# A two-layer decoder trunk in float32: four gated products of the feed-forwards, on GpSimd instead of VectorE

## The chip, the core and the metric

One core of one Trainium2 chip runs the whole program. The metric is the device time of one execution in microseconds (us), the median of several runs of the same program. The engines run side by side, each through its own queue in order, and wait for each other by semaphores: TensorE (PE, matrix products), VectorE (DVE), ScalarE (ACT), GpSimd (POOL) and SyncE (SP), which issues most of the transfers between HBM and the on-chip memory (SBUF). PE writes its results to PSUM.

## The reference

A sequence of 1024 tokens of width 1024 goes through two layers. Each has a token mixer (a gated linear recurrence in the first, sliding-window attention in the second) and then a gated feed-forward with a causal depthwise convolution of width 3. The change lies in the feed-forward alone:

```python
FFN_DIM = 2816
def conv_ffn(h, w_in, conv_w, conv_b, w_out):
    u = h @ w_in                                   # (S, 2 * FFN_DIM)
    u = causal_depthwise_conv(u, conv_w) + conv_b  # each column by itself, over 3 tokens
    a, b = jnp.split(u, 2, axis=-1)
    return (jax.nn.silu(a) * b) @ w_out
...
h = layer_norm(ALPHA * h + mix, ln_mix_g[layer], ln_mix_b[layer])
ff = conv_ffn(h, ffn_w_in[layer], ffn_conv_w[layer], ffn_conv_b[layer], ffn_w_out[layer])
h = layer_norm(ALPHA * h + ff, ln_ffn_g[layer], ln_ffn_b[layer])
```

The gated product is `silu(a) * b`.

## The kernel before

**The up-projection** (class `Up`, once per layer). The 5632 columns of `u` are made in 22 *chunk pairs* `fc`: 128 columns of `a` and the 128 columns of `b` that belong to them, for all 1024 tokens, with the columns on the partitions. A pair is a 2 x 2 block product made with seven block products (Strassen's scheme in Winograd's form) instead of eight. They are numbered, and run in the order 1, 2, 6, 7, 4, 5, 3; for pairs 0 and 1 they are interleaved and the products 4 and 5 come first, while layer norms of the last tokens are still under way. Each block product is 12 matmuls of 512 columns: four slices of the contraction, each in three passes (lines 194 to 196), since operands are split into a high part, which ACT makes by a cast (line 221), and a low part, the rest, which DVE subtracts (line 169). The third pass (L196) is the one that reads the low part of the weights.

**The weights of a pair** are loaded by SP (L416) into two of four raw buffers (rx0, rx1, rx2 and the last block of Y), split as they are (`weight_load`), then DVE forms the sums that the scheme needs (`weight_sums`, L425 to L428) and these are split in turn. The results lie in HL and HT. Even pairs use rx0 and rx1, odd pairs from 3 on rx2 and Y. So "L427 Y<-Y,rx2", "L428 rx2<-rx2,Y" and "L169 HL<-Y" belong to pair 3; that last one is the low part which its product 6 reads.

**Collecting a pair** (`collect`). Each block product is added from its PSUM bank into a tile C of Y (L451, L452 by ACT; L454 to L465 by DVE). After product 4 the half `a` is complete, after product 3 the half `b`. A complete half goes through the convolution: ACT makes its first tap with bias (L471), DVE adds the other two (L473, twice), for `a` ACT then takes silu (L476), and for `b` DVE multiplies the two halves (L478) and SP stores the product to HBM (L479, tile gd), where the down-projection fetches it. The half `a` lives in block 4 or 5 of Y (even or odd pair) until its store is done, the half `b` of every pair in block 6. So ACT's L471 for the next pair's `b` may only start when L478 has read block 6.

**PSUM.** A psmm tile is one bank; a psax tile is two banks. From pair 2 on the products go round eight banks, two of them in each psax tile.

**What sets the order.** PE's order is the order of the code. In the feed-forwards the orders of DVE, ACT, POOL and SP are made by a scheduler when the program is built, which estimates how long each instruction takes and places it by that; a change of one instruction's engine can therefore move others.

**GpSimd** has one operation in the feed-forwards: the power in the layer norm (L243, 128x1). Elsewhere it adds the bias in the attention (L1372, 128x512) and does one low part near the start (L169, 128x1024).

Of the kernel before, what the change touches and what calls it, by code (L numbers as in the profile page):

```python
# [14 lines left out]
ALU = mybir.AluOpType  # L15
# [92 lines left out]
def trunk(ctx: ExitStack, tc: tile.TileContext, a: dict, out: bass.AP):  # L108
    nc = tc.nc
# [232 lines left out]
    tt = nc.vector.tensor_tensor  # L342
# [6 lines left out]
    class Up:  # L349
# [97 lines left out]
        def collect(self, p, fc, ps):  # L447
            l, C = self.l, Y[:, 2 * (fc % 2):2 * (fc % 2) + 2, :]
            C11, C21, C12, C22 = C[:, 0, :512], C[:, 0, 512:], C[:, 1, :512], C[:, 1, 512:]
            if p == 1:  # L450
                nc.scalar.copy(C11, ps)  # L451
                nc.scalar.copy(C12, ps)  # L452
            elif p == 2:
                tt(C11, C11, ps, op=add)  # L454
            elif p == 6:
                tt(C12, C12, ps, op=add)
            elif p == 7:
                tt(C22, C12, ps, op=add)
            elif p == 4:
                tt(C21, C22, ps, op=add)  # L460
            elif p == 5:
                both = C[:, 1, :].rearrange("p (h n) -> p h n", h=2)
                tt(both, both, ps.unsqueeze(1).to_broadcast([P, 2, 512]), op=add)
            elif p == 3:
                tt(C12, C12, ps, op=add)  # L465
            if p in (4, 3):
                part = 0 if p == 4 else 1
                ci = fc + part * NF
                u, ca = C[:, part, :], Y[:, 4 + fc % 2, :]
                c = Y[:, 6, :] if part else ca  # L470
                nc.scalar.activation(c, u, AF.Identity, bias=cwt[:, l, 3, ci:ci + 1], scale=cwt[:, l, 2, ci:ci + 1])  # L471
                for sh in (1, 2):
                    nc.vector.scalar_tensor_tensor(c[:, sh:], u[:, :S - sh], cwt[:, l, 2 - sh, ci:ci + 1],  # L473
                                                   c[:, sh:], op0=ALU.mult, op1=ALU.add)
                if part == 0:
                    nc.scalar.activation(c, c, AF.Silu)  # L476
                else:
                    tt(ca, ca, c, op=ALU.mult)  # L478
                    nc.sync.dma_start(gd[:, fc, :], ca)  # L479

        def run(self, ready, down):
# [1080 lines left out]
```

## Time and profile before

| | |
|---|---|
| median of 3 runs | 2152.23 us (2151.32 to 2153.89) |
| the profiled execution | 2151.58 us |
| its span, first to last instruction | 2149.8 us |
| granted TensorE clock, mean | 0.999 |
| DVE, ACT, POOL: instructions | 2318, 1472, 143 |
| gated products (L478) on DVE | 44, 53.8 us in all, 1223 ns each |
| up-projection of layer 0, layer 1 | about 570 to 980 us, about 1520 to 1930 us |

How to read the rows below. The page gives each engine's busy time, and the span in 40 equal slices with the busy share of an engine in tenths. A row of who waits for whom has the engine and line that waited, the engine and line that ended the wait, the total, how many times, and the longest, in us. A row of the timeline has the start in us from the span's start, the duration in us, the engine, the line, the operation, what it writes and reads, the shape and the count; in brackets the idle time of that engine just before it and what ended it. PEld is PE's weight load, SPq a transfer's issue on SP. Matmuls overlap, so their start times tell more than their durations. A row of the chain of waits has the start, the time that this step has in the chain, and the instruction.

### The profile page before, as it was taken

To read this page: it belongs to the slowest core of one execution; us is meant where nothing else is said; L and a number is where in the kernel's file an instruction comes from. 1 tells how busy PE (TensorE), PEld (TensorE's weight loads), DVE (VectorE), ACT (ScalarE), POOL (GpSimd) and SP (SyncE) were. 2 spreads that over 40 slices of the span, in tenths; PEclk is the share of its full clock that TensorE was granted. 3 is DMA by queue.
4 is the path that set the end of the run, shared out by engine and by line. 5 is a ranking of instruction groups with operands and counts; after the bars stand their busy time and mean duration, and the time that the engine had idled before them with its cause. 6 is when DMAs were issued, how large, how long until landed. Compare 5 with 4: busy or idle time off the path is not lost.

```text
span 2149.8 us, 33060 instructions
## 1 busy us (share of the span) xinstructions
PE 2135.9 (99%) x13165; PEld 1809.0 (84%) x13165; DVE 1743.3 (81%) x2318; ACT 918.5 (43%) x1472; POOL 122.1 (6%) x143
## 2 busy tenths in 40 slices
PE   9999999999999999999999999999999999999998
PEld 9899999898888888888888888878888888888887
DVE  3877765577999999887978558969999899878986
ACT  3344434353444444434433256743544444444430
POOL 1000000001100000000001123311000000000002
PEclk9999999999999999999999999999999999999999
DMA  5755541123222222228854411133233222249662
GB/s 200 292 204 211 177 138 41 34 85 123 99 85 95 86 89 81 82 93 284 279 186 157 128 30 30 33 118 108 89 98 98 85 82 89 79 144 329 226 213 92
DMA packets 229842, 279.03 MB, mean 130 GB/s; under 512 B 29960, under 2 KB 158648, under 8 KB 226872
## 3 DMA queue, kind: packets, MB, share of 16 engines
q1 hardware_dynamic: 228736, 276.53, 38.5%
q8 instruction: 103, 1.69, 0.3%
q10 hardware_dynamic: 856, 0.37, 0.1%
q14 instruction: 51, 0.42, 0.1%
q0 software_dynamic: 96, 0.02, 0.0%
HBM read 213.94 MB, written 62.94 MB: 129 GB/s over the span
## 4 chain that ended last, share of the span: by engine, by line
PE 96%; DVE 2%; DMA 1%; issue 0%; ACT 0%; SPq 0%; DVEq 0%; ACTq 0%
PE psmm L194 20%; PE psmm L196 20%; PE psmm L195 20%; PE psax L194 9%; PE psax L196 9%; PE psax L195 9%; PE psax L200 3%; PE psmm L204 1%; PE psmm L200 1%; PE psax L204 1%; PE psax L1356 1%; DMA rx<-in_ffn_w_out_dram 1%; DVE T L169 0%; DVE Y L473 0%; PE psmm L688 0%
## 5 line engine op out<-in xcount | busy, mean ns | idle before, releaser
L194 PE MATMUL psmm<-T,HL 128*128 128x512 f32 x768 | 305.0, 397 | 0.0
L196 PE MATMUL psmm<-T,HL 128*128 128x512 f32 x768 | 299.4, 390 | 0.0
L195 PE MATMUL psmm<-T,HL 128*128 128x512 f32 x768 | 299.1, 389 | 0.0
L473 DVE SCALAR_TENSOR_TENSOR Y<-Y,cwt 128x1023 f32<-128x1023 f32 (+1 forms) x176 | 225.1, 1281 | 41.1 <-ACT Y L471 39.5
L221 ACT CAST HL<-rx 128x1024 fp32r<-128x1024 f32 (+1 forms) x151 | 152.0, 1009 | 200.8 <-PE psmm L195 46.9
L194 PE MATMUL psmm<-HL,T 128*128 128x256 f32 (+1 forms) x640 | 192.3, 300 | 0.9 <-issue 0.9
L196 PE MATMUL psmm<-HL,T 128*128 128x256 f32 (+1 forms) x640 | 189.8, 297 | 0.0
L195 PE MATMUL psmm<-HL,T 128*128 128x256 f32 (+1 forms) x640 | 189.6, 296 | 0.0
L169 DVE TENSOR_TENSOR HL<-rx,HL 128x1024 fp32r<-128x1024 f32 (+1 forms) x151 | 174.6, 1162 | 11.0 <-ACT HL L221 10.7
L196 PEld LDWEIGHTS psmm<-T,HL 128*128 128x128 f32 x768 | 144.1, 188 | 30.9
L194 PEld LDWEIGHTS psmm<-T,HL 128*128 128x128 f32 x768 | 144.3, 188 | 28.6
L195 PEld LDWEIGHTS psmm<-T,HL 128*128 128x128 f32 x768 | 144.4, 188 | 27.9
L471 ACT ACTIVATE Y<-Y,cwt 128x1024 f32<-128x1024 f32 x88 | 109.0, 1239 | 99.3 <-DVE Y L460 90.5
L194 PE MATMUL psax<-T,HL 128*128 128x512 f32 x352 | 137.3, 390 | 0.0
L196 PE MATMUL psax<-T,HL 128*128 128x512 f32 x352 | 137.0, 389 | 0.0
L195 PE MATMUL psax<-T,HL 128*128 128x512 f32 x352 | 137.0, 389 | 0.0
L195 PEld LDWEIGHTS psmm<-HL,T 128*128 128x128 f32 x640 | 122.3, 191 | 4.2 <-issue 1.0
L243 POOL TENSOR_TENSOR rs<-rs,nhalf 128x1 f32<-128x1 f32 x32 | 46.2, 1445 | 1398.7 <-DVE rs L242 1398.7
L194 PEld LDWEIGHTS psmm<-HL,T 128*128 128x128 f32 x640 | 122.3, 191 | 3.7 <-issue 0.4
L196 PEld LDWEIGHTS psmm<-HL,T 128*128 128x128 f32 x640 | 122.2, 191 | 3.5 <-DVE T L169 0.3
L169 DVE TENSOR_TENSOR HL<-raw,HL 128x1024 fp32r<-128x1024 f32 x51 | 62.2, 1222 | 71.9 <-ACT HL L176 71.8
L221 ACT CAST HT<-rx 128x1024 fp32r<-128x1024 f32 (+1 forms) x37 | 35.6, 962 | 113.9 <-DVE rx L427 74.3
(302 smaller groups left out, 5117.7 us busy)
## 6 DMA issues: line engine op xcount, KB each, us to landing
rx<-in_ffn_w_in_dram SPq DMA_DIRECT2D x136, 256.0 KB, 3.1
rx<-gd SPq DMA_DIRECT2D x118, 256.0 KB, 3.8
Y<-in_ffn_w_out_dram SPq DMA_DIRECT2D x44, 512.0 KB, 5.7
bsd<-Y SPq DMA_DIRECT2D x22, 1024.0 KB, 5.2
gd<-Y SPq DMA_DIRECT2D x44, 512.0 KB, 2.6
rx<-in_ffn_w_out_dram SPq DMA_DIRECT2D x54, 256.0 KB, 4.3
R<-bsd SPq DMA_DIRECT2D x44, 256.0 KB, 5.0
Y<-in_ffn_w_in_dram SPq DMA_DIRECT2D x40, 256.0 KB, 3.1
```

The source lines that it names most:

```text
L169: make = lambda e: e.tensor_tensor(lo, src, hi.bitcast(F32), op=ALU.subtract)
L194: nc.tensor.matmul(ps, st(0), mv(0), start=start, stop=False)
L195: nc.tensor.matmul(ps, st(0), mv(1), start=False, stop=False)
L196: nc.tensor.matmul(ps, st(1), mv(0), start=False, stop=stop)
L200: nc.tensor.matmul(ps, lhsT, rhs, start=start, stop=stop, **kw)
L204: nc.tensor.transpose(ps, src, ident)
L221: nc.scalar.copy(hi, src)
L243: nc.gpsimd.tensor_tensor(rs, rs, nhalf, op=ALU.pow)
L471: nc.scalar.activation(c, u, AF.Identity, bias=cwt[:, l, 3, ci:ci + 1], scale=cwt[:, l, 2, ci:ci + 1])
L473: nc.vector.scalar_tensor_tensor(c[:, sh:], u[:, :S - sh], cwt[:, l, 2 - sh, ci:ci + 1], c[:, sh:], op0=ALU.mult, op1=ALU.add)
L1356: nc.tensor.matmul(pv[:, e, jj, lo:], q[bp // 2][es, e, qs], Kl[es, pp, ks] if low else Kh[:, pp, e, ks], start=not low and jj == 0, stop= ...
```

## The change

The gated products of pairs 0 and 1 go to GpSimd, in both layers: four of 44. The operands, the tiles and the code's order stay.

```diff
@@ class Up: def collect(self, p, fc, ps):
                 if part == 0:
                     nc.scalar.activation(c, c, AF.Silu)
                 else:
-                    tt(ca, ca, c, op=ALU.mult)
+                    (nc.gpsimd if fc < 2 else nc.vector).tensor_tensor(ca, ca, c, op=ALU.mult)
                     nc.sync.dma_start(gd[:, fc, :], ca)
```

(`tt` is `nc.vector.tensor_tensor`.) The built programs differ in the two up-projections alone. PE's order is the same. On POOL, in each layer, the two products stand between the layer norms before and after the up-projection:

```order
 L1053 TENSOR_TENSOR ss<-ss,nhalf 128x8
-L243 TENSOR_TENSOR rs<-rs,nhalf 128x1 x16
+L243 TENSOR_TENSOR rs<-rs,nhalf 128x1 x8
+L478 TENSOR_TENSOR Y<-Y 128x1024 x2
+L243 TENSOR_TENSOR rs<-rs,nhalf 128x1 x8
 L1292 TENSOR_SCALAR sk<-sk 128x16
```

Two rows of POOL's queue become part of the up-projection, and nothing of GpSimd's own stands near them.

On DVE, in layer 0, the order before, from the second product (pair 1) to the third (pair 2). rx2_5425 is the raw buffer rx2; "L169 HL_83<-Y_82" is the low part that product 6 of pair 3 reads:

```order
L478 TENSOR_TENSOR Y_82<-Y_82 128x1024
L463 TENSOR_TENSOR Y_82<-Y_82,psmm_6070 128x1024
L473 SCALAR_TENSOR_TENSOR Y_82<-Y_82,cwt_77 128x1023
L465 TENSOR_TENSOR Y_82<-Y_82,psax_5969 128x512
L473 SCALAR_TENSOR_TENSOR Y_82<-Y_82,cwt_77 128x1022
L427 TENSOR_TENSOR Y_82<-Y_82,rx2_5425 128x512
L473 SCALAR_TENSOR_TENSOR Y_82<-Y_82,cwt_77 128x1023
L428 TENSOR_TENSOR rx2_5425<-rx2_5425,Y_82 128x512
L473 SCALAR_TENSOR_TENSOR Y_82<-Y_82,cwt_77 128x1022
L169 TENSOR_TENSOR HL_83<-Y_82,HL_83 128x1024
L478 TENSOR_TENSOR Y_82<-Y_82 128x1024
L169 TENSOR_TENSOR HL_83<-rx2_5425,HL_83 128x1024
```

And now, from L454 of pair 2, which both orders have at the same place:

```order
L454 TENSOR_TENSOR Y_82<-Y_82,psmm_6072 128x512
L169 TENSOR_TENSOR HT_5422<-Y_82,HT_5422 128x512
L456 TENSOR_TENSOR Y_82<-Y_82,psax_5969 128x512
L427 TENSOR_TENSOR Y_82<-Y_82,rx2_5425 128x512
L473 SCALAR_TENSOR_TENSOR Y_82<-Y_82,cwt_77 128x1023
L458 TENSOR_TENSOR Y_82<-Y_82,psax_5970 128x512
L473 SCALAR_TENSOR_TENSOR Y_82<-Y_82,cwt_77 128x1022
L428 TENSOR_TENSOR rx2_5425<-rx2_5425,Y_82 128x512
L460 TENSOR_TENSOR Y_82<-Y_82,psmm_6069 128x512
L169 TENSOR_TENSOR HL_83<-Y_82,HL_83 128x1024
L169 TENSOR_TENSOR HL_83<-rx2_5425,HL_83 128x1024
L473 SCALAR_TENSOR_TENSOR Y_82<-Y_82,cwt_77 128x1023
```

The sums of pair 3 (L427, L428) and both low parts of them stood after L465 of pair 2 and now stand ahead of its L463. The four convolution steps of pair 2 (L473) that stood ahead of the low part now stand behind it. The first split of pair 4's raw weights, which stood just after "L169 HT", has moved back behind L465.

On ACT, the order before at the same place ("x3" is three rows alike), beginning with L471 for the half `b` of pair 1:

```order
L471 ACTIVATE Y_82<-Y_82,cwt_77 128x1024 x3
L476 ACTIVATE Y_82<-Y_82 128x1024
L221 CAST HL_83<-Y_82 128x1024
L451 COPY Y_82<-psax_5970 128x512
L452 COPY Y_82<-psax_5970 128x512
L221 CAST HL_83<-rx2_5425 128x1024
L221 CAST HL_83<-Y_82 128x512
```

And now:

```order
L471 ACTIVATE Y_82<-Y_82,cwt_77 128x1024
L221 CAST HL_83<-Y_82 128x1024
L221 CAST HL_83<-rx2_5425 128x1024
L471 ACTIVATE Y_82<-Y_82,cwt_77 128x1024
L221 CAST HL_83<-Y_82 128x512
L476 ACTIVATE Y_82<-Y_82 128x1024
L471 ACTIVATE Y_82<-Y_82,cwt_77 128x1024
L451 COPY Y_82<-psax_5970 128x512
L452 COPY Y_82<-psax_5970 128x512
```

The casts for pair 3 have moved up, and the cast "HL<-Y 128x512", which needs the next load into Y (pair 5), now stands ahead of L476, of the last L471 and of the copies L451 and L452. On SP the loads into Y stand behind the store of the second product, as they did.

## The prediction

> **What bounds the kernel now.** I read the page first, then who waits for whom with TensorE (PE) alone, then the timeline of PE where it waits, then the chain of waits there.
>
> ```profile
> PE 2135.9 (99%) x13165; PEld 1809.0 (84%) x13165; DVE 1743.3 (81%) x2318; ACT 918.5 (43%) x1472; POOL 122.1 (6%) x143
> PE   9999999999999999999999999999999999999998
> DVE  3877765577999999887978558969999899878986
> ```
>
> PE is busy 99% of the span. VectorE (DVE) is busy 81% on average, but nine tenths and more in slices 10 to 15 and 27 to 30, which are the starts of the two up-projections. A busy DVE costs time only where PE has to wait for it:
>
> ```profile
> PE psmm L196 <- DVE HL L169: 1.6, 2, 0.8
> ...
> PE psax L194 <- DVE Y L594: 0.6, 1, 0.6
> ```
>
> Two waits for DVE, 0.8 us each, stand in the first row. PE's own timeline places them, one in each layer's up-projection:
>
> ```profile
> 628.09 0.39 PE L194 MATMUL psmm<-TX,HL 128*128 128x512 f32 x1
> 628.32 0.39 PE L195 MATMUL psmm<-TX,HL 128*128 128x512 f32 x1
> 629.52 0.50 PE L196 MATMUL psmm<-TX,HL 128*128 128x512 f32 x1 [0.81 <-DVE HL L169]
> 629.86 0.39 PE L194 MATMUL psmm<-TX,HL 128*128 128x512 f32 x1
> ```
> ```profile
> 1575.19 0.39 PE L195 MATMUL psmm<-TX,HL 128*128 128x512 f32 x1
> 1576.38 0.50 PE L196 MATMUL psmm<-TX,HL 128*128 128x512 f32 x1 [0.81 <-DVE HL L169]
> 1576.72 0.40 PE L194 MATMUL psmm<-TX,HL 128*128 128x512 f32 x1
> ```
>
> Matmuls start 0.23 us apart. The third matmul should have started at 628.55 and started at 629.52 (0.97 late); the next followed after 0.34 (0.11 more). The second layer shows the same, 0.96 and 0.11. So the delay is 1.6 us by the waits view and 2.15 us by the start times, for both layers together. This is product 6 of chunk pair 3; its third matmul reads the low part of a weight sum, which line 169 makes. The chain of waits shows what DVE did just before:
>
> ```profile
> 622.85 0.69 DVE Y L465
> 623.54 1.19 DVE Y L473
> 624.73 0.60 DVE Y L427
> 625.33 1.20 DVE Y L473
> 626.53 0.60 DVE rx L428
> 627.13 1.20 DVE Y L473
> 628.33 1.15 DVE HL L169
> 629.52 0.50 PE psmm L196
> ```
>
> The weight work of chunk pair 3 (L427, L428, L169) stands in DVE's queue between three convolution steps (L473), and the chain begins at L465, which waited for PE itself (its row is below). No L478 is in this chain. Taking L478 off DVE without moving anything else would therefore gain nothing: DVE would only wait longer at L465. Whatever is gained here comes from the order that is built around the moved products.
>
> **The change part by part.** It removes four DVE instructions (two per layer), adds four on GpSimd (POOL), and the scheduler writes DVE's and ACT's order anew from there to about chunk pair 6. PE's order is the same. What DVE and ACT did at this place, with the queue of loads on SP:
>
> ```profile
> 606.29 4.96 DVE L473 SCALAR_TENSOR_TENSOR Y<-Y,cwt 128x1023 f32<-128x1023 f32 x4
> 611.16 0.68 DVE L454 TENSOR_TENSOR Y<-Y,psmm 128x512 f32<-128x512 f32 x1
> 611.76 1.22 DVE L478 TENSOR_TENSOR Y<-Y 128x1024 f32<-128x1024 f32 x1
> 612.90 0.68 DVE L456 TENSOR_TENSOR Y<-Y,psax 128x512 f32<-128x512 f32 x1
> ...
> 614.10 1.22 DVE L169 TENSOR_TENSOR HL<-rx,HL 128x1024 fp32r<-128x1024 f32 x1
> 615.23 1.28 DVE L473 SCALAR_TENSOR_TENSOR Y<-Y,cwt 128x1023 f32<-128x1023 f32 x1
> ...
> 622.85 0.69 DVE L465 TENSOR_TENSOR Y<-Y,psax 128x512 f32<-128x512 f32 x1 [0.30 <-PE psax L196]
> ...
> 631.65 0.68 DVE L454 TENSOR_TENSOR Y<-Y,psmm 128x512 f32<-128x512 f32 x1
> ```
> ```profile
> 613.01 1.25 ACT L471 ACTIVATE Y<-Y,cwt 128x1024 f32<-128x1024 f32 x1 [1.09 <-DVE Y L478]
> ...
> 624.83 1.06 ACT L476 ACTIVATE Y<-Y 128x1024 f32<-128x1024 f32 x1
> ...
> 627.21 0.59 ACT L452 COPY Y<-psax 128x512 f32<-128x512 f32 x1
> ...
> 633.56 0.62 ACT L221 CAST HL<-Y 128x512 fp32r<-128x512 f32 x1 [4.82 <-DMA Y<-in_ffn_w_in_dram]
> ```
> ```profile
> 629.49 0.94 SPq L416 DMA_DIRECT2D Y<-in_ffn_w_in_dram  x2
> ```
>
> Price of one product on GpSimd. The trace has the very shape once, in a subtraction near the start, and it shows how long a hand-over to and from GpSimd takes:
>
> ```profile
> L169 POOL TENSOR_TENSOR HL<-raw,HL 128x1024 fp32r<-128x1024 f32 x1 | 2.4, 2367 | 1.9 <-DVE HL L677 1.9
> ```
> ```profile
> 562.10 0.14 DVE L242 TENSOR_SCALAR rs<-mv 128x1 f32<-128x1 f32 x1
> ...
> 562.39 1.45 POOL L243 TENSOR_TENSOR rs<-rs,nhalf 128x1 f32<-128x1 f32 x1 [5.26 <-DVE rs L242]
> ...
> 563.96 1.27 DVE L255 SCALAR_TENSOR_TENSOR Y<-Y,rs,rx 128x1024 f32<-128x1024 f32 x1
> ```
>
> So 2.37 us for a product (DVE: 1.22), 0.15 us from DVE's end to GpSimd's start (562.24 to 562.39), 0.12 back (563.84 to 563.96).
>
> Now the new order, walked with these rows. A DVE instruction holds the engine 1.13 us (128x1024), 0.60 (128x512) or 1.20 (L473), from start to start. DVE is at L454 at 611.16 as before. The convolution steps end at 611.25, so GpSimd's first product runs from 611.40 to 613.77. DVE meanwhile does L169 HT (611.76), L456 (612.36; its bank was finished before, since the old order ran it at 612.90 without a wait) and L427 (612.96), and is free at 613.56. The next L473 needs ACT's L471, which overwrites the tile that the product reads and was already waiting for L478 before (1.09 us). ACT now starts it at 613.89, 0.88 later than at 613.01, and ends at 615.14. So DVE idles 1.6 us and starts L473 at 615.17, the same time as before (615.23). This is where the change costs something, and the idle DVE hides it. Then L458 616.4, L473 617.0, L428 618.2, L460 618.8, and at 619.4 the low part that PE missed: it ends at 620.6. PE needs it at 628.55, so 7.9 us are in hand. The wait of 0.97 + 0.11 us goes, in both layers.
>
> What is late next? L465 frees a PSUM tile for product 7 of chunk pair 3, which PE reaches one product (12 matmuls, 2.7 us) after 628.1, at 630.8. From 619.4 DVE runs L169 twice, L473, L463, L473: 1.13 + 1.13 + 1.20 + 1.13 + 1.20 = 5.8, so L465 is at 625.2 and ends at 625.9, 4.9 us ahead. The second product starts after L473's end at 618.3: 618.4 to 620.8. Behind it on SP stand its store and then the two loads into Y (the same order as before). Those loads were issued at 629.49 and used by ACT at 633.56, 4.1 us later; now 621.3 and 625.4. ACT queues behind that cast (0.62) L476 (1.06), L471 (1.25) and the two copies L451 and L452 (0.59 each), 4.1 us in all, so to 629.5 at most. The copies free the PSUM tile that product 4 of chunk pair 3 writes, two products after product 6 and so at 633.5: 4.0 us in hand. The stores of the products themselves are read much later, by the down-projection. Nothing else becomes late, so the rest of the change is costed at nothing, as long as these three margins (7.9, 4.9, 4.0 us) hold.
>
> Further on the two layers' DVE work stays hidden as it is: it had 38.18 us of work in these 40 and now has 2.4 less.
>
> ```profile
> 600.00:640.00 40.00, 39.19 (x173) 32.15 (x172) 38.18 (x44) 19.69 (x22) 0.00 (x0) 1.00 0.27 89
> ```
>
> Sum: minus 1.6 (waits view) to minus 2.15 (start times). I take 2.0, nearer to the start times, since these are what the next matmuls follow. The profiled execution took 2151.58 us: 2149.6. The median of the three runs was 0.65 above that execution, so a median of the same kind would be 2150.2; I predict 2149.9.
>
> **The rivals.** *Contention at SBUF.* GpSimd reads two operands from SBUF while DVE does the same. The trace has only a short overlap of that kind:
>
> ```profile
> 1268.86 1.28 POOL L1372 TENSOR_TENSOR X<-X,bf 128x512 f32<-128x512 f32 x1 [7.11 <-DVE X L1364]
> ...
> 1270.00 0.70 DVE L1383 TENSOR_TENSOR X<-X,dn 128x512 f32<-128x512 f32 x1
> ```
>
> DVE started 0.14 us before GpSimd's row ends and took 0.70, against 0.68 for L456 of that size with nothing beside it: little sign of a hold, but also little overlap. Suppose DVE's two-input instructions wait for the whole product, of length d. Then L169 HT waits to 611.4 + d; three steps of 0.6, then L473, L458, L473 (3.0) and L428 (0.7) follow, so the second product starts at 617.0 + d and the missed low part at 617.0 + 2d. L465 ends 6.5 later, at 623.5 + 2d, against 630.8. At d = 2.37 it is 628.2, still 2.6 us early: the time stays 2149.6. From d = 3.65 on PE waits 2 us per us of d and layer. A product that also has to wait for one running DVE instruction (1.28) comes to 2.37 + 1.28 = 3.65, just at that point. If both engines ran at half speed, d = 4.7: 2 x 1.05 x 2 layers = 4.2 us, less the 2.0 gained: 2153.8. To be slower by more than 4.3 us, this must cost 6.3, so d must be 5.2 or more: 2156 and above. Without the hold the copies' margin decides (4.0 us, 2 per us of d): nothing up to d = 4.4, more than 4.3 us slower from 6.0. No row of GpSimd gives such a length.
>
> The Trainium skill ("SBUF — State Buffer", section Who interferes with whom) states exactly such a hold: a VectorE instruction with two SBUF inputs and a GpSimd instruction that reads SBUF exclude each other for their whole length, whoever starts second waits. By that rule the forecast still stands, with L465's margin 2.6 instead of 4.9 us; the 0.14 us of overlap above does not show it.
>
> *Another wait takes the place.* DVE now does the first split of chunk pair 4 late (it was at 614.10, now after L465, at 625.8) and its low parts in another order. Product 6 is the third of pair 3, so PE reaches pair 4 five products of 2.7 after 628.1, at 641.6, and over 14 us are in hand. Against it speaks also that DVE is ahead at the next L454: from L465's end at 625.8 it has L169 (1.13), L169 (0.60), L473, L425 (0.60) and L473 to do, so 630.5, where the old order came at 631.65. If such a wait came, it would be of the size of the old one: 2151.6, no change.
>
> *The gain is lost later.* After layer 0's up-projection PE waits once more (L594, 0.6 us in the second fence), behind loads and casts. If that stretch ran at its own pace, layer 0's share would go: 2150.6. The first load there is behind casts that follow PE's products, so it should shift with PE.
>
> *More than the two waits.* All of PE's idle time is 13.9 us (2149.8 less 2135.9), and elsewhere it is at other stages; a gain over 4.3 us has no row.
>
> **How the numbers follow.** The forecast 0.72, its own range 2148.8 to 2151.2; another wait 0.10 and the lost gain 0.07, both between 2150 and 2152; contention that costs time 0.08, of which 0.05 over 4.3 us; more gain 0.03. About 0.2%, 4.3 us, is what a measurement of this kernel can tell from no change, and the forecast is 0.1%. So faster 0.03, within 0.2% 0.92, slower 0.05. The range reaches from 2147.9 (the forecast less 0.9, which is how far the runs before lie below their median, and less one further wait of 1.1) to 2153.8, contention at half speed.
>
> **What would show it.** Right: no wait of L196 for DVE HL L169 near 629 and 1576; GpSimd rows L478 of 2.4 us, four of them; ACT's L471 after the first product waiting for POOL; a DVE gap of about 1.6 us before the L473 near 615; the low part from Y near 619. Wrong: L478 rows over 3.7 us, DVE's L169 stretched or late beside them, PE waiting for L465 or L452 at 630 to 634, or a span that differs by more than 4 us.

## The result, and the profile after

| | before | after |
|---|---|---|
| median | 2152.02 us (22 runs, 2150.42 to 2157.76) | 2149.27 us (22 runs, 2147.74 to 2153.09) |
| the profiled execution, its span | 2151.58, 2149.8 us | 2150.32, 2148.5 us |
| DVE busy, POOL busy | 1743.3, 122.1 us | 1743.4, 130.6 us |

The ratio is 0.9987, with a 95% interval of 0.9981 to 0.9993: the changed kernel is 2.75 us faster by the medians, 1.5 to 4.1 us by the interval. That is less than the 0.2% that a measurement of this kernel was taken to tell.

Who waits for whom, TensorE alone, in the changed kernel (engine, line and tile that waited, what ended the wait, total us, times, longest):

```profile
PE psmm L204 <- DVE T L169: 1.3, 1, 1.3
PE psmm L765 <- DVE Y L718: 1.0, 1, 1.0
PE psmm L194 <- issue: 0.8, 1, 0.8
PE psmm L688 <- DVE T L169: 0.5, 1, 0.5
PE psax L204 <- DMA Y<-in_x_dram: 0.5, 1, 0.5
PE psax L194 <- DVE Y L594: 0.5, 1, 0.5
```

The row "L196 <- DVE HL L169", which led this view before with 1.6 us, is gone. PE's timeline of the changed kernel shows product 6 of pair 3 in layer 0, with the matmuls 0.23 us apart and no wait at the third:

```profile
628.16 0.39 PE L194 MATMUL psmm<-TX,HL 128*128 128x512 f32 x1
628.39 0.39 PE L195 MATMUL psmm<-TX,HL 128*128 128x512 f32 x1
628.61 0.39 PE L196 MATMUL psmm<-TX,HL 128*128 128x512 f32 x1
```

The two traces hold the same 13165 matmuls in the same order, so each can be set against itself. In layer 0 the start times go from 0.07 us later than before to 1.04 us earlier at this matmul, and stay there to the end of the up-projection; in layer 1 they go from 0.77 to 1.87 us earlier at the same product. That is 1.11 + 1.10 = 2.2 us. All else together gives back 1.0 us, in steps of up to 0.6 us at loads, layer norms and the starts of the down-projections, where the experiments below step by other amounts and in both directions. So the spans differ by 1.3 us.

On the other engines less went as foretold. First POOL, then DVE in the changed kernel:

```profile
611.53 2.39 POOL L478 TENSOR_TENSOR Y<-Y 128x1024 f32<-128x1024 f32 x1 [42.40 <-DVE Y L473]
618.83 2.70 POOL L478 TENSOR_TENSOR Y<-Y 128x1024 f32<-128x1024 f32 x1 [4.91 <-DVE Y L473]
```
```profile
611.83 2.65 DVE L169 TENSOR_TENSOR HT<-Y,HT 128x512 fp32r<-128x512 f32 x1
614.40 0.67 DVE L456 TENSOR_TENSOR Y<-Y,psax 128x512 f32<-128x512 f32 x1
614.99 0.68 DVE L427 TENSOR_TENSOR Y<-Y,rx 128x512 f32<-128x512 f32 x1
615.60 1.27 DVE L473 SCALAR_TENSOR_TENSOR Y<-Y,cwt 128x1023 f32<-128x1023 f32 x1
...
618.58 0.68 DVE L428 TENSOR_TENSOR rx<-rx,Y 128x512 f32<-128x512 f32 x1
619.18 0.68 DVE L460 TENSOR_TENSOR Y<-Y,psmm 128x512 f32<-128x512 f32 x1
619.78 2.83 DVE L169 TENSOR_TENSOR HL<-Y,HL 128x1024 fp32r<-128x1024 f32 x1
...
627.19 0.67 DVE L465 TENSOR_TENSOR Y<-Y,psax 128x512 f32<-128x512 f32 x1
...
632.69 0.68 DVE L454 TENSOR_TENSOR Y<-Y,psmm 128x512 f32<-128x512 f32 x1
```

Two subtractions (L169) stand out: 2.65 us for 128x512 and 2.83 us for 128x1024, where the same shapes take 0.69 and 1.22 us elsewhere. Both were issued while a product ran on GpSimd, and each ended 0.56 and 1.08 us after that product did (614.48 against 613.92, 622.61 against 621.53): they did not run slowly, they were held until GpSimd had finished, and the hold counts as busy time in the row. L460, which stood beside the second product too, took its usual 0.68 us; one of its two inputs comes from PSUM, while both of L169's lie in SBUF. L428 was already running when the second product was issued at 618.83; it kept its 0.68 us and ended at 619.26, and the product took 2.70 us instead of 2.39, which is 2.27 from the end of L428.

So DVE was not relieved. In the same 40 us as in the prediction it is busier than before (there 38.18 us with 44 instructions):

```profile
600.00:640.00 40.00, 40.00 (x178) 33.10 (x178) 39.91 (x42) 19.82 (x22) 5.09 (x2) 1.00 0.27 90
```

The columns are PE, PEld, DVE, ACT and POOL busy, then the clock, the DMA share and GB/s. Over the whole span DVE's busy time is the same as before, although four products of 1.22 us have left it. The time came from the order.

### The profile page after: what moved, and what is told of

It reads as the page before. It is cut to its first block, busy times and chain, and to the rows that moved or that the text cites. A ratio compares the mean times of both kernels' runs of the same rounds, so it can differ in the third digit from the quotient of the medians.

```text
span 2148.5 us, 33071 instructions
## 1 busy us (share of the span) xinstructions
PE 2135.7 (99%) x13165; PEld 1808.9 (84%) x13165; DVE 1743.4 (81%) x2314; ACT 915.5 (43%) x1472; POOL 130.6 (6%) x147
## 5 line engine op out<-in xcount | busy, mean ns | idle before, releaser
L196 PE MATMUL psmm<-T,HL 128*128 128x512 f32 x768 | 299.3, 390 | 0.0
L473 DVE SCALAR_TENSOR_TENSOR Y<-Y,cwt 128x1023 f32<-128x1023 f32 (+1 forms) x176 | 225.2, 1281 | 43.3 <-ACT Y L471 41.8
L221 ACT CAST HL<-rx 128x1024 fp32r<-128x1024 f32 (+1 forms) x151 | 151.2, 1007 | 182.1 <-PE psmm L195 38.0
L196 PE MATMUL psmm<-HL,T 128*128 128x256 f32 (+1 forms) x640 | 189.7, 296 | 0.0
L169 DVE TENSOR_TENSOR HL<-rx,HL 128x1024 fp32r<-128x1024 f32 (+1 forms) x151 | 174.3, 1162 | 9.7 <-ACT HL L221 9.6
L196 PEld LDWEIGHTS psmm<-T,HL 128*128 128x128 f32 x768 | 144.1, 188 | 30.8
L471 ACT ACTIVATE Y<-Y,cwt 128x1024 f32<-128x1024 f32 x88 | 108.8, 1237 | 83.5 <-DVE Y L460 79.6
L196 PE MATMUL psax<-T,HL 128*128 128x512 f32 x352 | 137.0, 389 | 0.0
L196 PEld LDWEIGHTS psmm<-HL,T 128*128 128x128 f32 x640 | 122.2, 191 | 3.5 <-DVE T L169 0.3
L169 DVE TENSOR_TENSOR HL<-raw,HL 128x1024 fp32r<-128x1024 f32 x51 | 62.3, 1223 | 71.8 <-ACT HL L176 71.7
L221 ACT CAST HT<-rx 128x1024 fp32r<-128x1024 f32 (+1 forms) x37 | 35.5, 960 | 127.9 <-DVE rx L427 78.0
```

What stands on the lines that cost most here:

```text
L169: make = lambda e: e.tensor_tensor(lo, src, hi.bitcast(F32), op=ALU.subtract)
L196: nc.tensor.matmul(ps, st(1), mv(0), start=False, stop=stop)
L221: nc.scalar.copy(hi, src)
```

## The experiments

Nine kernels, each with runs of the kernel before on the same chip beside it. Theory: the gain is the order (the weight sum of pair 3 ahead of L465), and the product itself brings nothing, because its time comes back as a hold. Rival: DVE's relief is the gain.

**1. The order alone.** All products stay on DVE; the weight sums of pair 3 are given a higher priority in the scheduler.

```diff
-                if fc > 2:
-                    self.weights(fc)
+                if fc > 2: self.weight_load(fc)
+                with tc.high_priority(offset=60) if fc == 3 else nullcontext(): self.weight_sums(fc) if fc > 2 else None
```

> All 44 products stay on VectorE; only the scheduler's priority of pair 3's weight sums is raised, which brings its L427, L428 and the low part ahead of L465 of pair 2. Theory (the gain is the order): PE's two waits of L196 near 629 and 1576 go, and the time is about 2.0 us under before, like the change's. Rival (the gain is VectorE's relief by two products per layer): VectorE has as much to do as before, the waits or others of their size stay, and the time is that of before within 0.5 us.

Measured: 2149.85 us (11 runs; before 2151.95 in 23), ratio 0.9987, interval 0.9979 to 0.9996. The same gain with no product on GpSimd. DVE's timeline of this kernel shows the two moved steps, with L478 on DVE between them:

```profile
619.46 0.68 DVE L458 TENSOR_TENSOR Y<-Y,psax 128x512 f32<-128x512 f32 x1
620.06 1.22 DVE L478 TENSOR_TENSOR Y<-Y 128x1024 f32<-128x1024 f32 x1
621.20 0.68 DVE L428 TENSOR_TENSOR rx<-rx,Y 128x512 f32<-128x512 f32 x1
621.80 1.21 DVE L169 TENSOR_TENSOR HL<-Y,HL 128x1024 fp32r<-128x1024 f32 x1
```

The low part ends at 623.0, 0.4 us after the changed kernel's (622.61), and L169 of 128x1024 lasts 1.21 us. PE's starts step by 1.11 and 1.10 us at product 6, exactly as in the changed kernel. The order is enough.

**2. The products without the order.** The changed kernel, with the third sum of pair 3 kept behind L465 of pair 2.

```diff
-            tt(b22, b22, b11, op=sub)
+            with tc.issue_after(self.last_add.ins) if fc == 3 else nullcontext(): tt(b22, b22, b11, op=sub)
...
-                tt(C12, C12, ps, op=add)
+                self.last_add = tt(C12, C12, ps, op=add)
```

> As the change (four products on GpSimd), but L427 of pair 3 may not be issued ahead of L465 of pair 2, as it stood before. Rival (relief counts, and the hold of VectorE that the change's trace shows costs nothing): waits of 0.3 us are left, 1.3 us faster than before. Theory (order counts, and VectorE's two-input instructions wait for GpSimd's whole product): near 630 and 1577 PE waits first for ACT's copies, about 2.1 us, then for the low part, about 1.1 us, so 6.4 us in both layers in place of 2.0: about 4.5 us slower than before.

Measured: 2162.43 us (5 runs; before 2151.95), ratio 1.0046, interval 1.0034 to 1.0058: slower by 7 to 12 us. The rival falls: relieved of four products and without the early weight sum the kernel loses. DVE's timeline shows two holds ahead of L465, for subtractions that take 0.68 us without one:

```profile
612.24 2.64 DVE L169 TENSOR_TENSOR HT<-Y,HT 128x512 fp32r<-128x512 f32 x1
...
620.13 2.60 DVE L169 TENSOR_TENSOR HL<-rx,HL 128x512 fp32r<-128x512 f32 x1
...
627.49 0.68 DVE L465 TENSOR_TENSOR Y<-Y,psax 128x512 f32<-128x512 f32 x1
```

L465 comes 4.64 us later than before (622.85). The pin does not restore the whole order of before: one convolution step stands between L465 and the low part instead of three, so the low part starts 3.6 us after L465 (631.09) and not 5.5.

But the loss is about twice what I had worked out. PE's timeline of this kernel, at the same product:

```profile
627.99 0.39 PE L196 MATMUL psmm<-T,HL 128*128 128x512 f32 x1
630.84 0.80 PE L194 MATMUL psmm<-TX,HL 128*128 128x512 f32 x1 [2.47 <-ACT HL L221]
631.44 0.63 PE L195 MATMUL psmm<-TX,HL 128*128 128x512 f32 x1
632.36 0.79 PE L196 MATMUL psmm<-TX,HL 128*128 128x512 f32 x1 [0.29 <-DVE HL L169]
...
633.38 0.63 PE L195 MATMUL psmm<-TX,HL 128*128 128x512 f32 x1
633.80 0.63 PE L196 MATMUL psmm<-TX,HL 128*128 128x512 f32 x1
```

After the stall of 2.47 us and a second wait of 0.29 the matmuls stand 0.43 us apart instead of 0.23, with no wait between them. That lasts until 637.5, and PE's starts, 0.12 us later than before ahead of the stall, are 2.84 us later behind it and 5.22 us by 645. Layer 1 loses 5.5 us in the same way. The kernel before has its own delay of 1.08 us in that stretch. Set against the changed kernel, which has none there, layer 0 loses 6.2 us: 2.9 by the two waits, 3.3 by the wider spacing. Layer 1 loses 6.6: 3.3 and 3.3. So the waits came to 6.2 us in sum, near the 6.4 worked out, though most of it was for ACT's cast (L221) and not for its copies; the spacing is what was missing. Two costs were mixed: the holds, which make DVE late, and something that follows a long stall of PE. Experiments 5, 6 and 9 take them apart.

**3. All 44 products on GpSimd.**

```diff
-                    (nc.gpsimd if fc < 2 else nc.vector).tensor_tensor(ca, ca, c, op=ALU.mult)
+                    (nc.gpsimd if fc < 22 else nc.vector).tensor_tensor(ca, ca, c, op=ALU.mult)
```

> All 44 products on GpSimd, which takes 44 x 1.13 = 50 us off VectorE. Rival (relief): 2 us faster than before, or more. Theory (hold): each product keeps VectorE's next two-input instruction waiting for 1.6 to 2.0 us, more than the 1.13 saved; most of it is hidden, but PE waits about 0.6 us near 666 and 1602, 0.1 in some other pairs and about 2.3 us at the start of each down-projection, which waits for the last products: about 6 us slower than before (4 to 8).

Measured: 2161.0 us (6 runs; before 2151.95), ratio 1.0037, interval 1.0024 to 1.005: 5 to 11 us slower. If relief were the gain, this would be the fastest of all. The costliest group of DVE shows where the relief went (line, tiles and shape, count; busy us, mean ns; idle before it), first in the kernel before, then here:

```profile
L169 DVE TENSOR_TENSOR HL<-rx,HL 128x1024 fp32r<-128x1024 f32 (+1 forms) x151 | 174.6, 1162 | 11.0 <-ACT HL L221 10.7
```
```profile
L169 DVE TENSOR_TENSOR HL<-rx,HL 128x1024 fp32r<-128x1024 f32 (+1 forms) x151 | 240.1, 1598 | 13.1 <-ACT HL L221 13.0
```

53.8 us of products left DVE, and these 151 subtractions alone grew by 65.5 us; DVE is busy for 1768.7 us in all, against 1743.3. In this kernel's timeline 41 of DVE's L169 rows of 128x1024 begin while a product's row runs, and 40 of them end 1.08 or 1.09 us after it. The other began within 0.01 us of the product's row and kept its 1.22 us; there the product took 3.48 us instead of 2.39. PE loses 2.5 and 2.0 us net in the up-projections, and 3 and 4 us at L594 behind them, where it waits 2.0 and 2.2 us for DVE and then runs at the wider spacing of experiment 2. That wider spacing was not in the figures that I expected.

**4. One pair alone.** Two products on GpSimd, not four.

```diff
-                    (nc.gpsimd if fc < 2 else nc.vector).tensor_tensor(ca, ca, c, op=ALU.mult)
+                    (nc.gpsimd if fc < 1 else nc.vector).tensor_tensor(ca, ca, c, op=ALU.mult)
```

> Only pair 0's product on GpSimd (two in all). Rival (relief): half of the change's gain, about 1 us. Theory (order): the scheduler moves pair 3's low part ahead here too, so both waits go and the gain is the whole, about 2.0 us.

Measured: 2149.34 us (11 runs; before 2151.95), ratio 0.9986, interval 0.9978 to 0.9995. The whole gain. PE's starts step by 1.11 and 1.10 us at product 6; with the second product back on DVE the low part of pair 3 ends as late as 626.7, still 1.0 us before PE reads it.

**5. A somewhat longer stall.** The kernel before, with an in-place copy that delays the low part.

```diff
-                tt(C12, C12, ps, op=add)
+                tt(C12, C12, ps, op=add); [nc.vector.tensor_copy(C12, C12) for _ in range(1 if fc == 2 else 0)]
```

> The kernel before with one more DVE instruction per layer, an in-place copy of 128x512 after L465 of chunk pair 2, so that PE's stall at product 6 of chunk pair 3 grows from 0.81 us to about 1.2 to 1.6 us in each layer. Theory A (a stall costs what it lasts): 0.4 to 0.8 us more per layer, 2152.8 to 2153.6 us, granted clock 1.00 behind the stall. Theory B (every stall over about 1 us is followed by some microseconds at half the granted clock, as behind the stalls of 2.5 us in the pinned run): 2 us more per layer, 2156.5 to 2158 us. The trace of before has a stall of 1.4 us elsewhere with the clock at 1.00 behind it, so A is the likelier here.

Measured: 2154.31 us (11 runs) against 2154.01 for the kernel before on this chip (15 runs), ratio 0.9999, interval 0.999 to 1.0008. The stall of L196 grew to 1.13 us, by the start times 0.3 us more in layer 0 and 0.6 in layer 1, and nothing followed it; the clock (the last column but two) is full on both sides of it:

```profile
630.00:632.00 2.00, 1.08 (x5) 0.91 (x6) 2.00 (x3) 0.93 (x2) 0.00 (x0) 1.00 0.01 2
632.00:634.00 2.00, 2.00 (x10) 1.64 (x9) 2.00 (x3) 0.00 (x0) 0.00 (x0) 1.00 0.85 252
```

Theory A holds at this length; the stalls (1.13 and 1.11 us) came out a little shorter than I meant them to be.

**6. A long stall.** The kernel before, with the low part that PE waits for made twice.

```diff
-            split(blocks(2, 0), blocks(2, 1), r2)
+            split(blocks(2, 0), blocks(2, 1), r2); [low_part(blocks(2, 1), r2, blocks(2, 0), None) for _ in range(1 if fc == 3 else 0)]
```

> The kernel before with the low part that PE waits for made twice (the same result again, two DVE instructions of 128x1024 and one other later in the queue): PE's stall grows from 0.81 to about 4.3 us in each layer, 7.0 us in both. If a stall costs what it lasts: 2159.0 us, clock 0.999. If PE comes back at half the granted clock: each stall is followed by 4 to 7 us at 0.50, which adds 2 to 3.3 us, so 2163 to 2166 us and a mean clock of 0.995 to 0.997.

Measured: 2163.07 us (4 runs) against 2154.01, ratio 1.0046, interval 1.0033 to 1.006. In the trace PE's starts lose 5.6 us in layer 0 and 5.7 in layer 1. The stalls account for 3.4 and 3.7 of these, by the start times and beyond what they cost before; the other 4.1 us come behind them. The views by stretch of time of this kernel, around the stall in layer 0, which ends at 633.40:

```profile
626.00:630.00 4.00, 3.18 (x15) 2.29 (x13) 4.00 (x5) 3.21 (x5) 0.00 (x0) 1.00 0.00 0
630.00:632.00 2.00, 0.00 (x0) 0.00 (x0) 2.00 (x2) 0.00 (x0) 0.00 (x0) 0.81 0.05 20
632.00:634.00 2.00, 0.60 (x2) 0.51 (x3) 2.00 (x4) 0.00 (x0) 0.00 (x0) 0.50 0.78 273
634.00:636.00 2.00, 2.00 (x6) 1.61 (x5) 1.93 (x4) 0.00 (x0) 0.00 (x0) 0.50 1.07 315
636.00:638.00 2.00, 2.00 (x6) 1.52 (x6) 1.97 (x3) 1.83 (x2) 0.00 (x0) 0.50 0.61 176
638.00:640.00 2.00, 2.00 (x10) 1.64 (x9) 1.92 (x3) 1.64 (x3) 0.00 (x0) 0.98 0.01 3
```

The granted clock falls to 0.50 about 2 us into the stall (0.81 in a stretch of 2 us is 0.76 us at half) and comes back at about 638; PE does 6 matmuls in 2 us in place of 10, though it waits for nothing. That is the wider spacing of experiment 2, which doubled its loss.

**7. GpSimd work that reads less.** The changed kernel with a memset in place of the first product and a copy in place of the second; both products are left out.

```diff
+                    nc.gpsimd.memset(ca, 0.0) if fc == 0 else nc.gpsimd.tensor_copy(ca, c) if fc == 1 else tt(ca, ca, c, op=ALU.mult)
```

> The changed kernel with other GpSimd work in place of the two moved products: for chunk pair 0 a memset (it reads nothing), for chunk pair 1 a copy (it reads one operand); both products are left out. If what holds DVE's two-input instructions is that GpSimd reads SBUF, the rows beside the memset keep their length (L473 about 1.27 us, L169 of 128x512 0.69 us), and the two-input instruction that starts beside the copy (L427, normally 0.68 us) ends about 0.6 us after the copy's end. If any GpSimd work that writes SBUF holds them, the rows beside the memset are stretched too; if only two-operand work does, neither is. Time as the change's, 2148.5 to 2150.5 us, in all three cases.

Measured: 2149.69 us in one run. The memset tells nothing: it depended on less than the product did, ran early (605.45), and had only L463 and L465 beside it, which read PSUM. The copy does tell. POOL and DVE of this kernel:

```profile
617.38 1.04 POOL L478 COPY Y<-Y 128x1024 f32<-128x1024 f32 x1 [10.98 <-DVE Y L473]
```
```profile
617.12 0.68 DVE L458 TENSOR_TENSOR Y<-Y,psax 128x512 f32<-128x512 f32 x1
617.72 1.25 DVE L427 TENSOR_TENSOR Y<-Y,rx 128x512 f32<-128x512 f32 x1
```

L427, two inputs in SBUF, normally 0.68 us, took 1.25 and ended at 618.97, 0.55 us after the copy (618.42). So one operand read by GpSimd is enough to hold it.

**8. GpSimd work that only writes.** As 7, but both products become a memset of the tile that the product read, so that it starts where the product did and the order stays.

```diff
+                    nc.gpsimd.memset(c, 0.0) if fc < 2 else tt(ca, ca, c, op=ALU.mult)
```

> The changed kernel with a GpSimd memset of 128x1024 in place of each of the two moved products (both products are left out); it writes the tile that the product read, after the last convolution step, so it starts where the product started, and DVE's and ACT's orders are the changed kernel's. If DVE's two-input instructions are held only by GpSimd work that reads SBUF, the L169 of 128x512 and of 128x1024 beside the memsets last 0.69 and 1.22 us instead of 2.65 and 2.83. If work that only writes holds them too, they last until the memset's end (about 0.96 us after its start) and 0.6 or 1.1 us more: 1.2 us or more for the first. Time as the change's, 2148.5 to 2150.5 us, either way.

Measured: 2149.53 us in one run. POOL and DVE of this kernel:

```profile
611.62 0.96 POOL L478 MEMSET Y<- 128x1024 f32 x1 [42.38 <-DVE Y L473]
```
```profile
611.94 0.68 DVE L169 TENSOR_TENSOR HT<-Y,HT 128x512 fp32r<-128x512 f32 x1
```

The subtraction lay beside the memset for all but its last 0.04 us (611.94 to 612.62 beside 611.62 to 612.58) and took 0.68 us. Writing alone holds nothing. (The second memset was over before L169 of 128x1024 began.) PE's starts step by 1.11 and 1.10 us, as in the changed kernel: with and without holds the same.

**9. The pinned kernel without its holds.** Experiment 2 with the edit of 8:

```diff
-                    (nc.gpsimd if fc < 2 else nc.vector).tensor_tensor(ca, ca, c, op=ALU.mult)
+                    nc.gpsimd.memset(c, 0.0) if fc < 2 else tt(ca, ca, c, op=ALU.mult)
```

Both products are left out, and the orders of PE, DVE and ACT are those of experiment 2.

> The pinned kernel (the products moved, the weight sum of chunk pair 3 kept behind L465), with a memset in place of each moved product, DVE's, ACT's and PE's orders unchanged; both products are left out. If the pinned kernel lost its time to the two holds of about 2 us per layer, and then to the half clock behind PE's stalls, L465 of chunk pair 2 comes 4 us earlier (about 623.5), PE's stalls at product 6 of chunk pair 3 shrink from 2.5 us to 0.4 us or less, the clock stays at 1.00 there, and the time is 2149 to 2151 us. If the pinned order itself was the cause, the stalls stay and the time stays at 2159 to 2163 us.

Measured: 2149.49 us (11 runs; before 2151.83 in 15), ratio 0.9993, interval 0.9984 to 1.0002, against 2162.43 with the products. DVE's timeline of this kernel:

```profile
622.25 0.68 DVE L465 TENSOR_TENSOR Y<-Y,psax 128x512 f32<-128x512 f32 x1
...
625.86 1.22 DVE L169 TENSOR_TENSOR HL<-Y,HL 128x1024 fp32r<-128x1024 f32 x1
```

L465 comes at 622.25; in experiment 2 it came at 627.49 and this L169 at 631.09. Of these 5.2 us, 1.5 stood between the two kernels already at L454 (610.17 against 611.65); the other 3.8 are the two holds of 1.9 us. A memset is also shorter than a product, but in neither kernel does DVE's timeline show a wait between L454 and L465, so that has no part in it. The 12.9 us between the two kernels come from the holds beside four GpSimd instructions: first the hold, then the stall, then the clock. The run also limits experiment 2: with no hold the pinned order leaves PE one wait of 0.2 us. How much of that is DVE's relief and how much the two convolution steps that no longer stand ahead of the low part, no run shows.

## Why the prediction was right

The number, its range and the likeliest case came out as put down: 2149.27 against 2149.9, inside 2147.9 to 2153.8, and the difference within 0.2%. That the median came within 0.6 us of the forecast is partly luck: the gain is known to 1.5 to 4.1 us only, and the two profiled executions differ by 1.3. The mechanism, two waits of PE that the new order removes, is seen in the traces matmul by matmul.

- **"Whatever is gained here comes from the order."** Shown, by experiment 1 (order alone: the gain) and experiment 4 (half the moved work: the same gain). That taking L478 off DVE alone would gain nothing, since DVE would only wait longer at L465, was not tested by itself: no run has the old order without the products. By experiments 2 and 9 there is a stronger reason, which the prediction did not give here: GpSimd's reads take the time back, and more.
- **The sum, minus 1.6 to minus 2.15, 2.0 taken.** The start times were the right end: 1.11 + 1.10 = 2.2 us in the changed kernel, in experiments 1, 4 and 8 alike, against 1.08 and 1.07 read off before.
- **2.37 us per product.** 2.39 for the first, which had only L454, a reader of PSUM, beside it at its start. The second took 2.70; that it waited for L428 fits.
- **"DVE idles 1.6 us" after the first product.** Wrong in kind. DVE was held for 1.96 us (2.65 less 0.69) in L169 HT instead, the work walked for that time came behind it, and ACT's L471 (613.96, foretold 613.89) was done before DVE asked for it. The next L473 started at 615.60 instead of 615.17. The slack at this place in the queue went to the hold, and no gap was left.
- **"It had 38.18 us of work in these 40 and now has 2.4 less."** Wrong: it has 39.91, by the rows above. This is the step that failed. The overlap of 0.14 us that I took as "little sign of a hold" was too short to show one by itself. The trace of before has twelve rows of L1383 that start 0.14 to 0.18 us ahead of the end of a GpSimd row; all twelve end 0.55 us after it, where the held rows of the changed kernel end too, and the one with the longest overlap took 0.73 us instead of 0.69. Side by side they did show it.
- **The margins.** With the hold the walk gives the low part from 621.7 and L465 done at 628.2. Measured: the low part ran from 621.53, the end of the product, and L465 was done at 627.86, 3.0 us before PE needed its bank (630.88). The walk with the hold, kept as a rival, gave nearly these times; the forecast survived since neither walk used up the margins (7.9 became 6.0, 4.9 became 3.0, 4.0 became 2.9). ACT's cast of the next load came at 626.94 instead of 625.4, and L452 ended at 630.61 instead of 629.5, with PE's need at 633.5.
- **The rivals.** The hold came, at the price that left the time alone, and not at the price that costs. No other wait took the place of the one removed, although DVE was not ahead at the next L454 as I had it (632.69, not 630.5). The gain was not lost later in a piece; 0.5 us of layer 0's was even added at L594, and 0.6 us were lost there in layer 1.
- **What no part of the prediction priced** is the clock. Its line "PE waits 2 us per us of d and layer" took a stall to cost what it lasts. By experiments 2, 3 and 6 one of 2 us and more cost 1.6 to 3.3 us on top. Had the margins failed, the case of contention would have been too cheap by that.

## What to carry to other kernels

Before work is moved from DVE to GpSimd, look at what DVE does next: where it has two SBUF inputs, and GpSimd's instruction reads SBUF, it stands still for the whole of that instruction, which here is about twice as long (2.39 us for 1.22), and a net loss is likely; where it reads PSUM, the two do run side by side. If a scheduler builds the order, try the order alone: here a priority on one pair's weight sums gave the whole gain of the change. And a stall of TensorE of about 2 us or more should be priced at its length and, by the cases here, 1.6 to 3.3 us more, so a margin that runs out is dearer than it looks.

## What the runs showed of the hardware

**The hold** goes both ways and is full, not a slowdown: whoever comes second waits. DVE's L169 then ended 0.55 us (128x512) or 1.08 us (128x1024) after the GpSimd row, however long it had waited, and a GpSimd product that had to wait took 2.70 or 3.48 us instead of 2.39. It was seen beside a GpSimd product (two operands read) and a copy (one), not beside a memset (none), and only on DVE instructions with both inputs in SBUF. The Trainium skill ("SBUF — State Buffer", section Who interferes with whom) draws the line in the same place, at DVE's second SBUF input and GpSimd's reads; the rows here agree with it. Not expected was that the profile counts the hold as busy time of the waiting engine, with no idle time in brackets: only a duration that does not fit its shape gives it away.

**The clock behind a stall.** The shortest stall that was followed by half the clock is the one at L594 in layer 0 of experiment 3. PE had waited 1.97 us and was running again when the clock fell; the stretches of time of that kernel:

```profile
1042.00:1043.00 1.00, 0.40 (x2) 0.35 (x3) 1.00 (x2) 0.00 (x0) 0.00 (x0) 1.00 1.03 358
1043.00:1044.00 1.00, 1.00 (x4) 0.79 (x3) 1.00 (x2) 0.00 (x0) 0.00 (x0) 0.56 1.03 395
1044.00:1046.00 2.00, 2.00 (x6) 1.55 (x5) 2.00 (x5) 0.96 (x1) 0.00 (x0) 0.50 1.02 391
1046.00:1050.00 4.00, 4.00 (x17) 3.24 (x17) 3.86 (x6) 1.15 (x2) 0.00 (x0) 0.93 0.87 287
```

0.56 in 1 us is 0.88 us at half, 0.93 in 4 us is 0.56 us: half the clock from 1043.1 to 1046.6, about 3.4 us. In experiment 6 it was about 631.2 to 638, some 6.8 us, with a stall of 4.2 us. A stall of 1.13 us (experiment 5) was followed by nothing. The longest of the changed kernel (L204, 1.3 us) had the clock at 1.00 behind it, and between 1.3 and 1.97 us no run lies.

The traces record each change of the granted clock, more finely than this view, and the stretches between changes are whole multiples of 3.413 us in all eleven traces: 3.41 (1), 6.83 (2), 157.0 (46), 624.6 (183). So the clock changed only at the ends of steps of 3.41 us, and the idle time within one step is a better measure than the stall. Six steps at full clock in which PE idled for 1.97 to 2.58 us were followed by half the clock (experiments 2, 3 and 6); steps with up to 1.42 us of idle time were not. A step at half the clock without idle time was followed by the full clock, and one with 0.44 us or more by another at half. That explains why the clock fell 0.5 us after PE had resumed above (1042.60, the step's end at 1043.12), and why the price differs: 1.6 us for one step at half, 3.3 us for two (experiment 2), 2.0 to 2.3 us for two of which the stall itself fills a part (experiment 6). Whether a stall of 2 us that lies across the end of a step halves the clock, no run shows.

The Trainium skill ("TensorE: Matmul & The Clock Gate", section What's actually happening) tells of a window of about 3.4 us by which the clock is halved and restored; stretches of one and of two such windows agree with that. That it takes an idle window of that length, as the page has it, does not fit here, where 1.97 us of idle time sufficed.
